# Attention scores as 64-row matmuls of split q and k, two heads in turns on the two row halves, in a hybrid decoder trunk

## The chip, the cores and the metric

One Trainium2 chip, one core of it. The metric is device time of one execution in microseconds (us); the time before is the median of three runs. A profile is one more execution, with the hardware profiler on.

## What is computed

Two decoder layers over 512 tokens of width 1024, float32 in and out. In each layer: half a SwiGLU FFN, a token mixing, another half FFN, and a gated per-layer embedding. The change lies in the token mixing, whose three head groups read one projection of the normed input:

```python
def stick_breaking_attention(q, k, v):          # 4 heads x 64
    z = einsum('bqhd,bkhd->bhqk', qb, k) * scale
    log_beta = log_sigmoid(z)
    log_keep = where(mask, log_sigmoid(-z), 0.0)
    log_between = cumsum(log_keep, axis=3, reverse=True) - log_keep
    a = where(mask, exp(log_beta + log_between), 0.0)
    return einsum('bhqk,bkhd->bqhd', a, v)

def differential_attention(q, k, v, lam):       # 4 heads x 2 components x 64, v 128
    s = einsum('bqhcd,bkhcd->bchqk', qb, k) * scale
    pr = softmax(where(mask, s, -inf), axis=-1)
    attn = pr[:, 0] - lam * pr[:, 1]
    return einsum('bhqk,bkhe->bqhe', attn, v)

def causal_softmax_attention(q, k, v): ...      # 4 latent heads, 96 = 64 + 32 rotary

h = h + 0.5 * swiglu(rms_norm(h), ...)
h = h + concat(stick, diff, latent) @ w_out
h = h + 0.5 * swiglu(rms_norm(h), ...)
h = h + (p[i] @ w_ple_proj) * sigmoid(rms_norm(h) @ w_ple_gate)
```

## The kernel before

Activations stay transposed in SBUF, 128 channels by 512 tokens a tile, with the tokens in reverse order. A product of full precision is made of three fast matmuls (fp32r, one pass): every operand is split into a high part, rounded to fp32r (`whi`, `xh`), and the rest (`wlo`, `xl`), and `mm3` adds high x high, high x low and low x high in one PSUM bank. ScalarE mostly makes the high part, VectorE the low one. Matmuls of plain float32 operands take four passes; the profile has two instructions for each. Weights come in chunks of up to 512 KB on the DMA queue of SyncE (`raw<-in_wts`), two chunks ahead of their use, in one fixed order.

The token mixing is woven from generators ("threads"): `fill` runs the projections in the order `sb, df, sv, lat, dv, heads, o0, o2, pp, o6`; `scores` starts score stages, `values` takes finished weights, transposes them (`tr`) and joins them with v (`av`, `dav`). `weave` lets the first thread go on that a planner's clock (a table of costs: engines, 0.65 us a DMA plus 2.0 us until it lands) says can go on. That order is then the program: each engine runs its instructions in it. At most `WINDOW = 4` stages are under way, and score banks come from a pool of four PSUM banks (`bank2`).

A stage is one head and one tile of 128 queries `qt` (3, 2, 1, 0), which in the reversed order meets 128, 256, 384 or 512 keys. Stick-breaking heads (`sb_stage`): a mask on VectorE, two sigmoids on ScalarE (`run`, `beta`), a scan over `run`, and a product. Differential heads (`diff_stage`): two components, each masked (`e<-sc`), exponentiated, and combined.

Scores contract over only 64 channels. Before, the array's 128 rows hold the high part of q on 64 rows and the low part on the other 64; k's high part stands on both halves (`khh`) and so does its low part (`kll`). Two matmuls of 128 rows then give (qh+ql)(kh+kl):

```python
self.nc.tensor.matmul(o, qs[:, q0:q0 + P], khh[:, q0:], start=True, stop=False)
self.nc.tensor.matmul(o, qs[:, q0:q0 + P], kll[:, q0:], start=False, stop=True)
```

For that layout the stick-breaking heads are moved inside SBUF by DMA (`qs<-qh`, `kdup<-kh` and so on: 24 moves of 64 rows a layer, issued by SyncE). The differential heads go through DRAM: the projections' output columns are sorted so that a tile of 128 rows has 16 channels of all 8 components; the tiles are stored (`scratch<-dh`, `scratch<-dl`), and five loads a head (`dops<-scratch`, into three of five buffers of the pool `pairs`) bring q stacked and k twice. In `scores()`, loads of a head are issued one head before its first stage.

SyncE issues every one of these transfers in program order, and waits in it: a load whose buffer is still in use holds up the weight chunks behind it.

Of the kernel before, what the change touches and what calls it, by code (L numbers as in the profile page):

```python
# [87 lines left out]
def _layer_weights(z, l):  # L88

    def kt(w):  # L90
        return w.reshape(-1, P, w.shape[1]).transpose(1, 0, 2)

    gu = {1: kt(z['w_ffn1_gu'][l]), 2: kt(z['w_ffn2_gu'][l])}
    dn = {1: kt(z['w_ffn1_down'][l]), 2: kt(z['w_ffn2_down'][l])}


    order = (64 * np.arange(8)[None, :] + np.arange(64)[:, None]).reshape(-1)
    cols = np.arange(z['w_in'].shape[2])
    cols[768:1792] = 768 + np.concatenate([order, 512 + order])
    win, wout = kt(z['w_in'][l][:, cols]), kt(z['w_out'][l])  # L100
    pp, pg = kt(z['w_ple_proj'][l]), kt(z['w_ple_gate'][l])
    uq = z['mla_w_uq'][l].reshape(256, 4, 96)
    rot = uq[:, :, 64:].reshape(256, 2, 2, 2, 16).transpose(0, 1, 3, 2, 4)
    uq = kt(np.concatenate([uq[:, :, :64].reshape(256, 256), rot.reshape(256, 128)], axis=1))
    ukv = z['mla_w_ukv'][l].reshape(P, 4, 128)
    ukv = np.concatenate([ukv[:, :, :64].reshape(P, 256), ukv[:, :, 64:].reshape(P, 256)], axis=1)
    sv = np.concatenate([win[:, :, 512:768], win[:, :, 2688:2720]], axis=2)
    parts = []
    for key, cols in PLAN:
        t = key[0]  # L110
        if t in 'gv':
            c = key[2] * P + (FF if t == 'v' else 0)
            w = gu[key[1]][:, :, c:c + P]
        elif t == 'dn':
            _, n, lo, m, half = key
            k0, k1 = (lo, lo + 6) if half == 0 else (lo + 6, lo + 11)
            w = dn[n][:, k0:k1, m * P:(m + 1) * P]
        elif t == 'in':
            w = win[:, :, key[1]:key[1] + P]
        elif t == 'sv':  # L120
            w = sv[:, key[1]:key[2]]
        elif t == 'dv':
            w = win[:, key[1]:key[2], 1792:2304]
        elif t == 'uq':
            w = uq
        elif t == 'ukv':
            w = ukv
        elif t == 'out':
            _, k0, k1, m0, m1 = key
            w = wout[:, k0:k1, m0 * P:m1 * P]  # L130
        elif t == 'pp':
            w = pp[:, :, key[1] * P:key[2] * P]
        else:
# [18 lines left out]
def _constants():  # L152
    c = np.zeros((P, 8), np.float32)
    for r in range(P):
        c[r, 0] = INV_D[r % 64 // 8]
# [161 lines left out]
class Body:  # L317
# [371 lines left out]
                        yield 'go'  # L689
        return banks  # L690

    def stack_q(self, st, kind, q, h0):

        qh, ql = self.t2(dt=F32R, name='qh'), self.t2(dt=F32R, name='ql')
        self.split(qh, ql, q)

        def move():
            yield from self.when(qh, ql)
            for h in range(2):
                rows = slice(64 * h, 64 * h + 64)  # L700
                t = self.t2(dt=F32R, name='qs')
                self.move(t[0:64], qh[rows])
                self.move(t[64:128], ql[rows])
                st['q', kind, h0 + h] = t
        self.spawn(move())

    def stack_k(self, st, kind, k, h0):

        parts = self.t2(dt=F32R, name='kh'), self.t2(dt=F32R, name='kl')
        self.split(parts[0], parts[1], k)  # L710

        def move():
            yield from self.when(*parts)
            for h in range(2):
                rows = slice(64 * h, 64 * h + 64)
                dup = []
                for p in parts:
                    t = self.t2(dt=F32R, name='kdup')
                    self.move(t[0:64], p[rows])
                    self.move(t[64:128], p[rows])  # L720
                    dup.append(t)
                st['k', kind, h0 + h] = dup
        self.spawn(move())

    def scores(self, st, kind, h, qt):
        while ('q', kind, h) not in st or ('k', kind, h) not in st:
            yield 'blocked'
        qs, (khh, kll) = st['q', kind, h], st['k', kind, h]
        yield from self.when(qs, khh, kll)
        yield from self.room('bank2')  # L730
        ps = self.bank2('sc', hold=True)
        q0 = qt * P
        o = ps[:, 0:S - q0]
        self.nc.tensor.matmul(o, qs[:, q0:q0 + P], khh[:, q0:], start=True, stop=False)
        self.nc.tensor.matmul(o, qs[:, q0:q0 + P], kll[:, q0:], start=False, stop=True)
        return o

    def transposed(self, at, qt, a):

# [129 lines left out]

    def diff_qk(self, l, x, st):  # L870

        st['scratch'] = s = self.dram.tile([2, 2, 64, 8, S], F32, name='scratch', tag='scratch')
        for m in range(4):
            for i, c in enumerate((768, 1280)):
                box = []
# [10 lines left out]
    def store(self, s, m, i, parts, st):  # L886
        yield from self.when(*parts)
        for p, t in enumerate(parts):
            self.move(s[i, p, 16 * m:16 * m + 16].rearrange('d c t -> (d c) t'), t)
        st['stored'] = st.get('stored', 0) + 1  # L890

    def diff_ops(self, st, h):


        s, hc = st['scratch'], slice(2 * h, 2 * h + 2)
        a, b = slice(0, 64), slice(64, P)
# [4 lines left out]
        for c in range(2):  # L901
            st['q', 'df', 2 * h + c], st['k', 'df', 2 * h + c] = q[:, c], (kh[:, c], kl[:, c])

    def out_proj(self, l, k0, k1, mixed, nxt=None):
        step = 8 // (k1 - k0)
# [36 lines left out]
                yield 'go'  # L942


    def sb_stage(self, st, h, qt):
        nc = self.nc
        n = S - qt * P
        z = yield from self.scores(st, 'sb', h, qt)
        nc.vector.tensor_tensor(out=z[:, 0:P], in0=z[:, 0:P], in1=self.m_strict, op=ALU.add)
        run, beta = self.st2(name='run')[:, 0:n], self.st2(name='beta')[:, 0:n]  # L950
        self.act(run, z, AF.Sigmoid, scale=-0.125)
        self.act(beta, z, AF.Sigmoid, scale=0.125)
        self.done(z)

        yield from self.when(run)
        nc.vector.tensor_tensor_scan(run, run, run, 1.0, ALU.mult, ALU.min)
        yield from self.when(beta)
        nc.vector.tensor_tensor(out=beta[:, 1:n], in0=beta[:, 1:n], in1=run[:, 0:n - 1], op=ALU.mult)
        st['weights', 'sb', h, qt] = beta

    def diff_stage(self, st, l, h, qt):
        nc = self.nc
        n = S - qt * P
        z = []
        for c in range(2):
            ps = yield from self.scores(st, 'df', 2 * h + c, qt)
            z.append(self.masked(ps, n, 0.125))
# [128 lines left out]
    def mixing(self, l, norm, nxt):  # L1096
# [4 lines left out]
        def start():  # L1101
            r = None
            for c in range(4):
# [6 lines left out]
                (self.stack_q, self.stack_k)[c // 2](st, 'sb', t, 2 * (c % 2))  # L1110

            st['rope'] = []
            for tab in self.rope_d:
# [30 lines left out]
                self.done(banks[t])  # L1144
            st['dv'] = dv

        stages = [(kind, h, qt) for kind in KINDS for h in range(4) for qt in (3, 2, 1, 0)]
        under_way = []

        def scores():  # L1150

            for kind, h, qt in stages:
                while len(under_way) >= WINDOW:
                    yield 'blocked'
                if kind == 'sb':
                    stage = self.sb_stage(st, h, qt)
                elif kind == 'df':
                    while st.get('stored') != 8:
                        yield 'blocked'
                    for i in range(min(h + 2, 4) if qt == 3 else 0):  # L1160
                        if ('q', 'df', 2 * i) not in st:
# [12 lines left out]

        def values():

            for kind, h, qt in stages:
                while ('weights', kind, h, qt) not in st:
                    yield 'blocked'
                if qt == 3:  # L1180
                    at = self.quad(dt=F32, name='at')
                yield from self.transposed(at, qt, st.pop(('weights', kind, h, qt)))
                under_way.pop(0)
                yield 'go'
                if qt == 0:
                    if kind == 'df':
                        finish = self.diff_finish(st, h, at)
                    elif h % 2 == 0:
                        even = at
                        continue  # L1190
                    else:
                        finish = self.join_heads(st, h - 1, (even, at), 'vs' if kind == 'sb' else 'vm',
                                                 0 if kind == 'sb' else 6)
                    self.spawn(finish, values)
                    yield 'go'

# [98 lines left out]
```

## Time and profile before

| what | value |
|---|---|
| median of 3 runs | 2057.83 us (2054.44 to 2058.54) |
| profiled execution | 2062.05 us |
| span of that profile | 2060.2 us |
| TensorE matmuls busy | 2029.0 us, 98% |
| VectorE busy | 1112.5 us, 54% |
| ScalarE busy | 793.1 us, 38% |
| mean DMA rate | 107 GB/s |
| mixing, layer 0 | about 369 to 613 us of the span |
| mixing, layer 1 | about 1385 to 1629 us of the span |

The profiled execution's own time has 1.85 us around the span. Names in the rows are tiles: `sc` a score bank, `pt` a projection into transposed layout, `pn` one into natural layout (values), `tr` a transpose of weights, `wo` the output projection, `msc` a latent head's score. All instructions go through one recording helper, so all have its line (L238), and DMA issues have L447 or L455. The start of a matmul is recorded, and its end is modelled with the array's latency in it, so that the time a matmul takes is read as the distance from its start to the start of the next one. fp32r shows as f32 in the matmuls' rows.

### The profile page before, as it was taken

The numbers are of one execution on the slowest core, as the hardware profiler recorded it, in microseconds if no ns is written. First come the engines' busy times: TensorE is split into PE (matmuls) and PEld (weight loads), VectorE is DVE, ScalarE is ACT, GpSimd is POOL, SyncE is SP. The second block draws the span as 40 slices with busy tenths as digits, with TensorE's granted clock in tenths as the row PEclk, the third lists the DMA queues.
The fourth block names the chain that finished last, engine by engine and source line by source line (L and its number), as shares of the span: only waits on it lengthen the run. The fifth ranks groups of instructions, "written<-read, shape, count | busy, mean of one in ns | idle before, by whom it ended". The sixth has DMA issues, their size and how long they took to land.

```text
span 2060.2 us, 23527 instructions
## 1 busy us (share of the span) xinstructions
PE 2029.0 (98%) x9148; PEld 1656.6 (80%) x9148; DVE 1112.5 (54%) x1762; ACT 793.1 (38%) x1275; POOL 5.1 (0%) x13
## 2 busy tenths in 40 slices
PE   8999999999999999999999999999999999999997
PEld 6888888887778888888888888888776788888885
DVE  6743444677756443444754334457686654344446
ACT  5422333445654222333543223335466433222343
POOL 0000000000000000000000000000000000000000
PEclk9999999999999999999999999999999999999998
DMA  4323233565323323333333233336633232333232
GB/s 167 101 86 108 94 94 91 156 193 142 92 87 92 98 85 107 99 90 97 101 95 100 85 110 92 93 102 175 191 110 104 81 103 90 91 106 103 85 107 75
DMA packets 73663, 220.34 MB, mean 107 GB/s; under 512 B 9024, under 2 KB 9024, under 8 KB 73552
## 3 DMA queue, kind: packets, MB, share of 16 engines
q1 hardware_dynamic: 73040, 217.23, 35.2%
q0 software_dynamic: 512, 1.61, 0.3%
q8 instruction: 72, 1.18, 0.2%
q14 instruction: 39, 0.32, 0.1%
HBM read 197.83 MB, written 10.49 MB: 101 GB/s over the span
## 4 chain that ended last, share of the span: by engine, by line
PE 93%; DMA 3%; DVE 2%; ACT 1%; issue 0%; SPq 0%; DVEq 0%
PE g L238 23%; PE v L238 23%; PE dn L238 23%; PE pt L238 6%; PE pg L238 4%; PE wo L238 3%; PE pn L238 2%; PE sc L238 1%; PE tr L238 1%; DMA dops<-scratch 1%; PE pp L238 1%; PE av L238 1%; DMA raw<-in_wts 1%; PE msc L238 1%; PE dav L238 1%; PE sum L238 1%
## 5 line engine op out<-in xcount | busy, mean ns | idle before, releaser
L238 ACT CAST whi<-raw 128x1024 fp32r<-128x1024 f32 (+3 forms) x363 | 346.1, 954 | 950.6 <-PE dn L238 295.2
L238 DVE TENSOR_TENSOR wlo<-raw,whi 128x1024 fp32r<-128x1024 f32 (+2 forms) x388 | 427.9, 1103 | 223.3 <-ACT whi L238 222.6
L238 PE MATMUL g<-xh,whi 128*128 128x512 f32 x704 | 276.8, 393 | 6.5 <-ACT xh L238 6.5
L238 PE MATMUL g<-xl,whi 128*128 128x512 f32 x704 | 274.9, 390 | 0.5 <-DVE xl L238 0.5
L238 PE MATMUL g<-xh,wlo 128*128 128x512 f32 x704 | 274.7, 390 | 0.0
L238 PE MATMUL v<-xh,whi 128*128 128x512 f32 x704 | 273.9, 389 | 0.0
L238 PE MATMUL v<-xh,wlo 128*128 128x512 f32 x704 | 273.9, 389 | 0.0
L238 PE MATMUL v<-xl,whi 128*128 128x512 f32 x704 | 273.9, 389 | 0.0
L238 PE MATMUL dn<-hh,whi 128*128 128x512 f32 x704 | 273.9, 389 | 0.0
L238 PE MATMUL dn<-hl,whi 128*128 128x512 f32 x704 | 273.9, 389 | 0.0
L238 PE MATMUL dn<-hh,wlo 128*128 128x512 f32 x704 | 273.9, 389 | 0.0
L238 DVE TENSOR_TENSOR v<-v,rt 128x512 f32<-128x512 f32 x88 | 60.8, 690 | 260.8 <-PE v L238 260.8
L238 PEld LDWEIGHTS g<-xh,whi 128*128 128x128 f32 x704 | 132.7, 188 | 35.0 <-ACT xh L238 6.8
L238 PEld LDWEIGHTS g<-xl,whi 128*128 128x128 f32 x704 | 132.7, 189 | 29.9 <-DVE xl L238 1.3
L238 PEld LDWEIGHTS g<-xh,wlo 128*128 128x128 f32 x704 | 132.6, 188 | 27.5
L238 PEld LDWEIGHTS dn<-hl,whi 128*128 128x128 f32 x704 | 132.2, 188 | 27.5
L238 PEld LDWEIGHTS v<-xh,wlo 128*128 128x128 f32 x704 | 132.2, 188 | 27.6 <-DVE wlo L238 0.2
L238 PEld LDWEIGHTS v<-xl,whi 128*128 128x128 f32 x704 | 132.2, 188 | 27.5
L238 PEld LDWEIGHTS dn<-hh,whi 128*128 128x128 f32 x704 | 132.2, 188 | 27.4
L238 PEld LDWEIGHTS v<-xh,whi 128*128 128x128 f32 x704 | 132.2, 188 | 27.3
L238 PEld LDWEIGHTS dn<-hh,wlo 128*128 128x128 f32 x704 | 132.2, 188 | 27.3
L238 DVE TENSOR_TENSOR g<-g,rt 128x512 f32<-128x512 f32 x88 | 60.8, 690 | 172.1 <-PE g L238 172.0
(196 smaller groups left out, 2581.7 us busy)
## 6 DMA issues: line engine op xcount, KB each, us to landing
raw<-in_wts SPq DMA_DIRECT2D x250, 512.0 KB, 3.5
raw<-in_wts SPq DMA_DIRECT2D x66, 384.0 KB, 3.0
raw<-in_wts SPq DMA_DIRECT2D x64, 320.0 KB, 2.9
dops<-scratch SPq DMA_DIRECT2D x32, 256.0 KB, 4.9
scratch<-dh SPq DMA_DIRECT2D x16, 256.0 KB, 2.9
scratch<-dl SPq DMA_DIRECT2D x16, 256.0 KB, 3.8
dops<-scratch SPq DMA_DIRECT2D x8, 512.0 KB, 7.6
res<-in_xT SPq DMA_DIRECT2D x8, 256.0 KB, 5.3
```

Source lines behind the costliest of these rows:

```text
L238: r = f(*args, **kw)
```

## The change

The scores of two stick-breaking heads (a pair), or of the two components of a differential head, are made together. q and k are split as before, but nothing is stacked: the two heads stand on rows 0 to 63 and 64 to 127 of the same four tiles `qh, ql, kh, kl`. Each score is three matmuls of 64 rows, qh kh, qh kl and ql kh, and the two heads take turns, each on its own half of the rows and into its own bank. The term ql kl is no longer made.

```diff
-    def stack_q(self, st, kind, q, h0):
...
-    def stack_k(self, st, kind, k, h0):
...
+    def split_pair(self, st, which, kind, pair, t):
+        parts = self.t2(dt=F32R, name=which + 'h'), self.t2(dt=F32R, name=which + 'l')
+        self.split(*parts, t)
+        st[which, kind, pair] = parts
+
+    def scores(self, st, kind, pair, qt):
...
+        (qh, ql), (kh, kl) = st['q', kind, pair], st['k', kind, pair]
+        yield from self.when(qh, ql, kh, kl)
+        while len(self.held['bank2']) > BANKS['bank2'] - 2:
+            yield 'blocked'
         q0 = qt * P
-        o = ps[:, 0:S - q0]
-        self.nc.tensor.matmul(o, qs[:, q0:q0 + P], khh[:, q0:], start=True, stop=False)
-        self.nc.tensor.matmul(o, qs[:, q0:q0 + P], kll[:, q0:], start=False, stop=True)
-        return o
+        out = []
+        for i in range(2):
+            yield from self.room('bank2')
+            out.append(self.bank2('sc', hold=True)[:, 0:S - q0])
+        for p, (q, k) in enumerate(((qh, kh), (qh, kl), (ql, kh))):
+            for i, o in enumerate(out):
+                rows = slice(64 * i, 64 * i + 64)
+                self.nc.tensor.matmul(o, q[rows, q0:q0 + P], k[rows, q0:], start=p == 0, stop=p == 2)
+        return out
```

The 24 moves a layer are gone. The scratch tensor is now ordered by component first, the columns of `w_in` are sorted to fit, and a differential head has two tiles (q, k) with the high part in one half of the columns and the low part in the other, filled by four loads of 256 KB:

```diff
-        st['scratch'] = s = self.dram.tile([2, 2, 64, 8, S], F32, name='scratch', tag='scratch')
+        st['scratch'] = s = self.dram.tile([2, 2, 8, 64, S], F32, name='scratch', tag='scratch')
...
-        q, kh, kl = (self.pairs.tile([P, 2, S], F32R, name='dops', tag='pr') for _ in range(3))
-        self.move(q, s[0, :, :, hc].rearrange('p d c t -> (p d) c t'))
-        for t, half, p in ((kh, a, 0), (kh, b, 0), (kl, a, 1), (kl, b, 1)):
-            self.move(t[half], s[1, p, :, hc])
+        for i, which in enumerate('qk'):
+            t = self.pairs.tile([P, 2, S], F32R, name='dops', tag='pr')
+            for p in range(2):
+                self.move(t[:, p], s[i, p, 2 * h:2 * h + 2].rearrange('c d t -> (c d) t'))
+            st[which, 'df', h] = t[:, 0], t[:, 1]
```

A stick-breaking stage now does a pair (mask and sigmoids of both, then scan and product of both), counts as two in the window of four, and `values` transposes both heads of it before it frees its place.

On TensorE, the first scores of layer 0 (`pt` is the projection of the stick-breaking k and of the first differential tile). Before, the high halves of one head's four stages, and a few matmuls later the low halves:

```order
L238 MATMUL pt<-xh,wlo 128x512
L238 MATMUL sc<-kdup,qs 128x128
L238 MATMUL sc<-kdup,qs 128x256
L238 MATMUL sc<-kdup,qs 128x384
L238 MATMUL sc<-kdup,qs 128x512
L238 MATMUL pt<-xh,whi 128x512
```

and in the changed kernel two pair stages, one directly behind the other (x2 is one matmul of each head):

```order
L240 MATMUL pt<-xh,wlo 128x512
L240 MATMUL sc<-kh,qh 128x128 x2
L240 MATMUL sc<-kl,qh 128x128 x2
L240 MATMUL sc<-kh,ql 128x128 x2
L240 MATMUL sc<-kh,qh 128x256 x2
L240 MATMUL sc<-kl,qh 128x256 x2
L240 MATMUL sc<-kh,ql 128x256 x2
L240 MATMUL pt<-xh,whi 128x512
```

The pair's scores stand some 30 `pt` matmuls earlier than the first scores did. In the whole program the 48 pair stages stand in 36 unbroken blocks: 12 of them are directly behind another.

On VectorE, behind the second block of that first pair (384 and 512 keys), in the changed kernel: the split of the last stick-breaking k, a weight chunk and the two rotary tables (`rot`) come first, then masks (`sc<-sc`), scans (`run<-run`) and products (`beta`) of both heads:

```order
L240 TENSOR_TENSOR sbqk<-pt,rt 128x512
L240 TENSOR_TENSOR wlo<-raw,whi 128x1024
L240 TENSOR_TENSOR kl<-sbqk,kh 128x512
L240 TENSOR_TENSOR rot<-cos_427,rt 128x512
L240 TENSOR_TENSOR rot<-sin_425,rt 128x512
L240 COPY rt<-rt 128x4
L240 TENSOR_TENSOR sc<-sc,cst 128x128 x2
L240 SCALAR_TENSOR_TENSOR run<-run 128x384
```

Before, one head's scans of 128, 256 and 384 keys follow each other in this place, with the `rot` rows ahead of the first of them.

On SyncE's queue, from the last store of the differential q and k on. Before (64x1024 is half a tile of k):

```order
L447 DMA dops<-scratch 128x1024
L447 DMA scratch<-dh 128x512
L455 DMA raw<-in_wts 128x1024
L447 DMA scratch<-dl 128x512
L447 DMA dops<-scratch 64x1024 x4
L447 DMA dops<-scratch 128x1024
L447 DMA dops<-scratch 64x1024 x4
L455 DMA raw<-in_wts 128x1024 x2
```

and now:

```order
L449 DMA dops<-scratch 128x512 x2
L449 DMA scratch<-dh 8x16x512
L457 DMA raw<-in_wts 128x1024
L449 DMA scratch<-dl 8x16x512
L449 DMA dops<-scratch 128x512 x6
L457 DMA raw<-in_wts 128x1024
L449 DMA dops<-scratch 128x512 x2
L457 DMA raw<-in_wts 128x1024
L449 DMA dops<-scratch 128x512 x4
```

Behind the last store, nine loads stood ahead of the next weight chunk, the last two of them into a buffer that the first head still read; now six stand there, all into free buffers, and the four of the last row (k of the third head, q of the fourth) wait for the first head's.

## Rows read from the trace of the kernel before

**Rows 1.** The page: busy time by engine, and the chain that ended last by engine.

```profile
PE 2029.0 (98%) x9148; PEld 1656.6 (80%) x9148; DVE 1112.5 (54%) x1762; ACT 793.1 (38%) x1275; POOL 5.1 (0%) x13
...
PE 93%; DMA 3%; DVE 2%; ACT 1%; issue 0%; SPq 0%; DVEq 0%
```

**Rows 2.** Groups by line and shape, TensorE: stick-breaking score matmuls of one width.

```profile
L238 PE MATMUL sc<-kdup,qs 128*128 128x512 f32 x16 | 5.9, 428 | 0.0
```

**Rows 3.** Timeline of TensorE around the first scores: start us, us, instruction.

```profile
396.72 0.80 PE L238 MATMUL sc<-kdup,qs 128*128 128x128 f32 x4
397.36 0.39 PE L238 MATMUL pt<-xh,whi 128*128 128x512 f32 x1
```

**Rows 4.** Timeline of TensorE: differential heads' values, four heads of 128 output columns.

```profile
530.06 8.80 PE L238 MATMUL dav<-at,dv 128*128 128x512 f32 x32
538.61 0.48 PE L238 MATMUL uq<-ch,whi 128*128 128x512 f32 x1
```

**Rows 5.** Timeline of TensorE: latent values, two heads of 64 output columns in turns.

```profile
573.15 0.40 PE L238 MATMUL wo<-mh,wlo 128*128 128x512 f32 x1
573.47 2.38 PE L238 MATMUL av<-at,vm 128*64 128x512 f32 x16
575.78 0.50 PE L238 MATMUL wo<-mh,whi 128*128 128x512 f32 x1
576.12 0.39 PE L238 MATMUL wo<-ml,whi 128*128 128x512 f32 x1
```

**Rows 6.** Timelines of TensorE, 10 ns and then 3 us: four matmuls of 32 rows.

```profile
556.31 0.70 PE L238 MATMUL drr<-rt,cst 32*128 32x512 f32 x2
...
556.31 1.98 PE L238 MATMUL drr<-rt,cst 32*128 32x512 f32 x8
```

**Rows 7.** Timelines of TensorE and its weight loads, inside a full-array stretch.

```profile
542.56 0.39 PE L238 MATMUL uk<-ch,wlo 128*128 128x512 f32 x1
542.78 0.28 PE L238 MATMUL uv<-whi,ch 128*128 128x256 f32 x1
...
542.56 0.19 PEld L238 LDWEIGHTS uv<-whi,ch 128*128 128x128 f32 x1
```

**Rows 8.** Timelines of TensorE: waits for differential loads, layer 0, then layer 1.

```profile
460.35 3.08 PE L238 MATMUL sc<-dops 128*128 128x128 f32 x12 [1.77 <-DMA dops<-scratch]
...
488.00 0.41 PE L238 MATMUL sc<-dops 128*128 128x128 f32 x2 [1.86 <-DMA dops<-scratch]
...
1476.68 0.70 PE L238 MATMUL sc<-dops 128*128 128x128 f32 x4 [0.43 <-DMA dops<-scratch]
1479.51 3.86 PE L238 MATMUL sc<-dops 128*128 128x128 f32 x12 [2.13 <-DMA dops<-scratch]
...
1505.63 0.41 PE L238 MATMUL sc<-dops 128*128 128x128 f32 x2 [0.56 <-DMA dops<-scratch]
```

**Rows 9.** Busy time by stretch: PE, PEld, DVE, ACT, POOL; granted clock; DMA share; GB/s.

```profile
460.00:466.00 6.00, 5.65 (x25) 5.14 (x26) 3.46 (x16) 1.81 (x8) 0.00 (x0) 0.72 0.78 201
488.00:494.00 6.00, 6.00 (x25) 5.37 (x26) 3.40 (x16) 4.18 (x14) 0.00 (x0) 0.72 0.64 141
1479.00:1484.00 5.00, 4.49 (x18) 4.24 (x19) 3.54 (x15) 0.20 (x1) 0.00 (x0) 0.66 0.48 103
```

**Rows 10.** The chain that ended last, 440 to 500 us: start us, us, what.

```profile
445.00 1.28 ACT L360
...
448.22 0.69 DVE dl L238
...
448.93 5.96 DMA scratch<-dl
...
455.45 4.77 DMA dops<-scratch
```

**Rows 11.** Timelines: TensorE's wait for a stick-breaking product, and VectorE's scans.

```profile
405.47 0.52 PE L238 MATMUL tr<-cst,beta 128*128 128x128 f32 x3 [0.38 <-DVE beta L238]
...
403.71 0.95 DVE L238 TENSOR_TENSOR_SCAN run<-run 128x384 f32<-128x384 f32 x1
```

More of the change, by code (lines that the diff above doesn't have):

```diff
@@ L94, in _layer_weights @@
     dn = {1: kt(z['w_ffn1_down'][l]), 2: kt(z['w_ffn2_down'][l])}
-    order = (64 * np.arange(8)[None, :] + np.arange(64)[:, None]).reshape(-1)
+    order = [64 * np.arange(8)[:, None] + d + np.arange(n)[None, :] for d, n in
+             ((0, 8), (8, 8), (16, 16), (32, 16), (48, 16))]
+    order = np.concatenate([o.reshape(-1) for o in order])
     cols = np.arange(z['w_in'].shape[2])
@@ L154, in _constants @@
     for r in range(P):
-        c[r, 0] = INV_D[r % 64 // 8]
+        c[r, 0] = INV_D[r % 8]
         c[r, 1] = -1.0 if r < 64 else 1.0
@@ L690, in proj_n @@
         return banks
-    def stack_q(self, st, kind, q, h0):
[L694 to L705, printed above, removed]
@@ L707, in stack_k @@
-    def stack_k(self, st, kind, k, h0):
[L709 to L723, printed above, removed]
@@ L725, in scores @@
-    def scores(self, st, kind, h, qt):
-        while ('q', kind, h) not in st or ('k', kind, h) not in st:
+    def split_pair(self, st, which, kind, pair, t):
[3 more added lines that the diff above has]
+    def scores(self, st, kind, pair, qt):
+        while ('q', kind, pair) not in st or ('k', kind, pair) not in st:
             yield 'blocked'
[L728 to L731, printed above, removed]
+        (qh, ql), (kh, kl) = st['q', kind, pair], st['k', kind, pair]
+        yield from self.when(qh, ql, kh, kl)
+        while len(self.held['bank2']) > BANKS['bank2'] - 2:
+            yield 'blocked'
@@ L888, in store @@
         for p, t in enumerate(parts):
-            self.move(s[i, p, 16 * m:16 * m + 16].rearrange('d c t -> (d c) t'), t)
+            if m == 0:
+                self.move(s[i, p, :, 0:8], t[0:64])
+                self.move(s[i, p, :, 8:16], t[64:128])
+            else:
+                self.move(s[i, p, :, 16 * m:16 * m + 16], t)
         st['stored'] = st.get('stored', 0) + 1
     def diff_ops(self, st, h):
-        s, hc = st['scratch'], slice(2 * h, 2 * h + 2)
-        a, b = slice(0, 64), slice(64, P)
-        q, kh, kl = (self.pairs.tile([P, 2, S], F32R, name='dops', tag='pr') for _ in range(3))
-        self.move(q, s[0, :, :, hc].rearrange('p d c t -> (p d) c t'))
-        for t, half, p in ((kh, a, 0), (kh, b, 0), (kl, a, 1), (kl, b, 1)):
-            self.move(t[half], s[1, p, :, hc])
-        for c in range(2):
-            st['q', 'df', 2 * h + c], st['k', 'df', 2 * h + c] = q[:, c], (kh[:, c], kl[:, c])
+        s = st['scratch']
+        for i, which in enumerate('qk'):
[3 more added lines that the diff above has]
+            st[which, 'df', h] = t[:, 0], t[:, 1]
     def out_proj(self, l, k0, k1, mixed, nxt=None):
@@ L942, in ple_proj, with sb_stage @@
                 yield 'go'
-    def sb_stage(self, st, h, qt):
+    def sb_stage(self, st, pair, qt):
         nc = self.nc
         n = S - qt * P
[L948 to L959, printed above, removed]
+        banks = yield from self.scores(st, 'sb', pair, qt)
+        sticks = []
+        for z in banks:
+            nc.vector.tensor_tensor(out=z[:, 0:P], in0=z[:, 0:P], in1=self.m_strict, op=ALU.add)
+            run, beta = self.st2(name='run')[:, 0:n], self.st2(name='beta')[:, 0:n]
+            self.act(run, z, AF.Sigmoid, scale=-0.125)
+            self.act(beta, z, AF.Sigmoid, scale=0.125)
+            self.done(z)
+            sticks.append((run, beta))
+        for i, (run, beta) in enumerate(sticks):
+            yield from self.when(run)
+            nc.vector.tensor_tensor_scan(run, run, run, 1.0, ALU.mult, ALU.min)
+            yield from self.when(beta)
+            nc.vector.tensor_tensor(out=beta[:, 1:n], in0=beta[:, 1:n], in1=run[:, 0:n - 1], op=ALU.mult)
+            st['weights', 'sb', 2 * pair + i, qt] = beta
     def diff_stage(self, st, l, h, qt):
@@ L963, in diff_stage @@
         n = S - qt * P
[L964 to L967, printed above, removed]
+        banks = yield from self.scores(st, 'df', h, qt)
+        z = [self.masked(ps, n, 0.125) for ps in banks]
         sm, r = self.sm(2, name='sum'), self.sm(2, name='rec')
@@ L1109, in start @@
                 nc.vector.tensor_tensor(out=t, in0=box[0], in1=r, op=ALU.mult)
-                (self.stack_q, self.stack_k)[c // 2](st, 'sb', t, 2 * (c % 2))
+                self.split_pair(st, 'qk'[c // 2], 'sb', c % 2, t)
             st['rope'] = []
@@ L1145, in diff_v @@
             st['dv'] = dv
-        stages = [(kind, h, qt) for kind in KINDS for h in range(4) for qt in (3, 2, 1, 0)]
+        stages = [(kind, h, qt) for kind in KINDS for h in range(2 if kind == 'sb' else 4) for qt in (3, 2, 1, 0)]
         under_way = []
@@ L1152, in scores @@
             for kind, h, qt in stages:
-                while len(under_way) >= WINDOW:
+                while sum(1 + (k == 'sb') for k, _, _ in under_way) >= WINDOW:
                     yield 'blocked'
@@ L1160, in scores @@
                     for i in range(min(h + 2, 4) if qt == 3 else 0):
-                        if ('q', 'df', 2 * i) not in st:
+                        if ('q', 'df', i) not in st:
                             self.diff_ops(st, i)
@@ L1175, in values @@
         def values():
[L1177 to L1182, printed above, removed]
+            ats = {}
+            for kind, i, qt in stages:
+                for h in ((2 * i, 2 * i + 1) if kind == 'sb' else (i,)):
+                    while ('weights', kind, h, qt) not in st:
+                        yield 'blocked'
+                    if qt == 3:
+                        ats[h] = self.quad(dt=F32, name='at')
+                    yield from self.transposed(ats[h], qt, st.pop(('weights', kind, h, qt)))
                 under_way.pop(0)
                 yield 'go'
-                if qt == 0:
+                if qt == 0 and (kind == 'df' or h % 2 == 1):
                     if kind == 'df':
[L1187 to L1190, printed above, removed]
-                    else:
-                        finish = self.join_heads(st, h - 1, (even, at), 'vs' if kind == 'sb' else 'vm',
-                                                 0 if kind == 'sb' else 6)
+                        finish = self.diff_finish(st, h, ats.pop(h))
+                    else:
+                        finish = self.join_heads(st, h - 1, (ats.pop(h - 1), ats.pop(h)),
+                                                 'vs' if kind == 'sb' else 'vm', 0 if kind == 'sb' else 6)
                     self.spawn(finish, values)
```

## The prediction

> **What bounds the kernel now.** I read the page first. TensorE's matmuls are busy for 98% of the span, and the chain that ended last lies on TensorE for 93% of it [rows 1]. So a change pays only what it takes from TensorE's own stream of matmuls, or from the places where that stream waits. I therefore looked for the price of the score matmuls (the groups by shape and the timeline around them), for what a change of tile shape costs in this trace (the stretches where other matmuls already use part of the array), and for TensorE's waits in the two mixing stages with their granted clock. What the other engines do is read only where TensorE waits for them.
>
> **1. The score matmuls.** The stick-breaking heads have 16 of each width [rows 2], the differential ones with eight components instead of four heads twice as many, so there are 48 sets of the four widths (a set: the high or the low half of one head's four stages). One set took 397.36 - 396.72 = 0.64 us on TensorE, with plain matmuls right ahead and behind [rows 3]. Before, that is 48 x 0.64 = 30.7 us. Afterwards each of the 24 pairs of heads or components (2 stick-breaking and 4 differential a layer, so 12 over both layers) needs three sets for each of its two heads, 72 sets in all. If the two row halves run side by side, they take the time of 36: 23.0 us, **7.7 us less**. If they do not, 72 x 0.64 = 46.1 us, 15.4 us more.
>
> Do they run side by side? The trace has no 64-row matmul, but two near ones. In the latent values two heads use 64 columns each in turns: 16 instructions in 575.78 - 573.47 = 2.31 us [rows 5]; one differential head of the same lengths at full width took (538.61 - 530.06)/4 = 2.14 us [rows 4]. Two heads cost about as much as one. And the four 32-row matmuls of the sub-norm, nearest in kind, started two within 10 ns and ended after 1.98 us [rows 6]; one 512-wide plain matmul is 2.14 x 512/1280 = 0.86 us, so four in sequence would be 3.4 us. I take full overlap.
>
> **2. Going into and out of the split array.** This has a price in the same rows. The matmul ahead of the `av` block takes 573.47 - 573.15 = 0.32 us and the one behind it 0.34 us [rows 5], where a matmul in a plain stretch takes 542.78 - 542.56 = 0.22 us [rows 7]; the block itself is 2.31 - 2.14 = 0.17 us too long. Together 0.10 + 0.12 + 0.17 = 0.39 us for each visit. The `drr` block gives 1.98 - 2 x 0.86 = 0.26 us inside alone. The 48 pair stages stand in 36 unbroken blocks, so I add 36 x 0.39 = **14.0 us**. Bounds: 0.17 us a visit if only the inner part is paid (6.1 us), 0.50 us if the wider weights of 128 columns show twice (18 us). That this is more than the matmuls save is the main point against the change.
>
> Does a weight load still hide inside a block, where each half gets new weights for every pass? In a plain stretch the next weights start loading at 542.56 while a matmul over the same 128 rows starts in that very instant, and the next matmul follows 0.22 us later [rows 7]: hidden. The Trainium skill says otherwise (TensorE: Matmul & The Clock Gate, Part 3, "The mechanism"): a weight load overlaps a matmul in flight only where their row groups differ. By that, the second and third pass of each half would wait for their own load; the price of it is worked out as a rival. The sum goes by the row.
>
> **3. Waits for the differential loads.** TensorE stood 1.77 + 1.86 + 0.43 + 2.13 + 0.56 = 6.75 us for `dops<-scratch` [rows 8]. After three of these waits its granted clock fell from 2.4 to 1.2 GHz for a while: the mean was 0.72 over 6 us twice and 0.66 over 5 us once [rows 9], which cost 1.7 us each time, 5.1 us in all. So late loads cost 11.8 us.
>
> The waits are of two kinds. The 1.86 and the 0.56 are the third head's: with three of five buffers to a head, its last tile could only be loaded when the second head was done. With two tiles a head its q finds a free buffer and its k needs only the first head's, one head of work earlier. These 2.4 us, and one fall of the clock, go. The others are the first head's. The chain to them ran through a table load on ScalarE (1.28), the low half of the last projection, its store (5.96 from issue to landing) and the load of k's low part (4.77) [rows 10]. Now the stick-breaking stages are over sooner and the table load stands ahead of the last projections; k's low part is one transfer of 256 KB instead of two, and 256 KB less is in flight beside the store (an estimate from the 5.96: 1 us off). That is 1.3 + 0.5 + 1 = 2.8 us off a chain that was 1.8 us late. But about nine transposes that stood between the last projection and these scores are gone too, so TensorE arrives about 1 us sooner. Balance: just in time. I leave 0.5 us a layer and no fall of the clock: **10.8 us less**. Bounds: 11.8 (no wait), 4.1 (the first head as late as before: 2.4 + 1.7).
>
> The 24 moves a layer that go were not waited for by TensorE (other matmuls filled the time, [rows 3] shows scores right behind projections); I give them nothing. Fewer matmuls' operands, the extra halves of two stores a layer and the finer planner window cost nothing that a row shows: TensorE has projections in front of every one of those.
>
> **4. The stick-breaking chain.** Before, TensorE waited 0.38 us for a product (`beta`) once a layer; VectorE's scan of 384 keys alone takes 0.95 us [rows 11]. Now both heads' scans and products follow each other, twice the work between a pair's scores and its last transpose, and for the second block of the first pair VectorE first does five full-width instructions (`dl` of that width takes 0.69 us [rows 10]; a weight chunk is twice as wide), some 4 us. TensorE has 12 projections, 12 x 0.22 = 2.7 us, before it wants the first of these products. In the second pair many more projections stand between. I expect two waits of under 1 us in each layer, **2.4 us more** in all than now. Bounds: 0 (VectorE catches up) and 6.
>
> **Sum:** -7.7 + 14.0 - 10.8 + 2.4 = -2.1 us. The profiled execution's own time is 2062.05 us (its span 2060.2 and 1.85 around it), so 2060.0; it was 4.2 us slower than the median of the runs, 2057.83, which gives 2055.7 us. About 0.2% (4.1 us) is what a measurement of this kernel can tell from no change.
>
> **Rivals.**
> *The switches cost less.* If only the inner 0.17 us is paid where weights for the other half are loaded ahead, the second term is 6.1: -10.0 us, 2047.8. For it: the 0.10 and 0.12 in [rows 5] may belong to the change from fast to plain matmuls, which scores don't make. Against: `drr` with plain matmuls on its outer side still shows 0.26 inside.
> *The first head's loads stay late.* Place: the first `dops` scores of each layer. They keep 1.77 + 0.43 + 2.13 us and two falls of the clock, 7.7 instead of 1.0: +4.6 us, 2062.4, slower. It decides once k's low part lands some 2 us after TensorE comes.
> *The pair's scans hold up TensorE.* 3 us of waits a layer and a fall of the clock each (1.7): 9.4 instead of 2.4, +4.9 us, 2062.7.
> *The halves do not overlap.* +15.4 instead of -7.7: +21 us, 2078.8. [rows 6] speak against it.
> *Weights wait for their own half.* Two of three loads in 48 stages and two heads side by side, each at most the 0.19 us of a load in [rows 7]: up to 96 x 0.19 = 18 us more, 2074. This is what the Trainium skill's rule above would do; [rows 7] contradict it.
>
> **How the numbers follow.** Chances: the sum as forecast 0.52, with a range of its own of 2051 to 2061 from the bounds of the terms 3 and 4 (0.18 of it faster, 0.34 within 0.2%); cheaper switches 0.20 (faster); late loads 0.12 (0.05 the same, 0.07 slower); scans 0.08 (0.02 and 0.06); no overlap 0.05; weights 0.03. Faster 0.38, same 0.41, slower 0.21. The range from 2046 to 2065 takes in the first four cases and leaves the last two and the tails, under 2 in 10.
>
> **What the profile of the changed kernel would show.** Term 1: the two heads' score matmuls start within some 10 ns, and the six of 512 keys take about 0.7 us. Term 2: the matmul ahead of a block and the first behind it take about 0.3 instead of 0.22 us. Term 3: no wait for `dops` over 1 us, none at all at the third head, and no stretch at the lower clock in the mixing. Term 4: short waits of transposes for `beta` behind the first pair's second block. I am wrong if blocks cost clearly other than 0.4 us, if scores run one half after the other, or if new waits bring the clock down.

## The result, and the profile after

The changed kernel took 2070.24 us (median of 4 runs, 2068.86 to 2070.45) where the one before took 2058.07 in the same comparison: ratio 1.0067, 95% interval 1.0055 to 1.0080. It is 12 us slower by these medians, 14 by the ratio, which is not the quotient of the two medians; the prediction said 2055.7 and its range ended at 2065. The profiled execution of the changed kernel took 2070.45 us, 8.4 more than that of the kernel before.

The page after, busy time of TensorE and the chain that ended last, as in [rows 1]:

```profile
PE 2033.9 (98%) x9244; PEld 1648.6 (80%) x9244; DVE 1112.1 (54%) x1752; ACT 799.5 (39%) x1285; POOL 5.1 (0%) x13
...
PE 93%; DVE 3%; DMA 2%; ACT 1%; issue 0%; SPq 0%; DVEq 0%
```

TensorE still sets the time, so again only its stream and its waits count. A block of stick-breaking scores of 512 keys between projections, timeline of TensorE (start us, us, instruction), answers to [rows 3, 5]:

```profile
424.37 0.40 PE L240 MATMUL pt<-xh,wlo 128*128 128x512 f32 x1
424.70 0.51 PE L240 MATMUL sc<-kh,qh 64*128 64x512 f32 x2
425.04 0.40 PE L240 MATMUL sc<-kl,qh 64*128 64x512 f32 x2
425.28 0.40 PE L240 MATMUL sc<-kh,ql 64*128 64x512 f32 x2
425.61 0.50 PE L240 MATMUL pt<-xh,whi 128*128 128x512 f32 x1
425.94 0.39 PE L240 MATMUL pt<-xl,whi 128*128 128x512 f32 x1
```

Read the starts. Each line of scores is both heads' matmul of one pass, and the middle pass takes 425.28 - 425.04 = 0.24 us, the time of one full-width matmul: the halves run side by side. The matmul ahead takes 0.33, the block 425.61 - 424.70 = 0.91, the matmul behind 0.33; three passes and two matmuls of 0.23 would be 1.15, so the visit costs 0.42 us.

The waits of TensorE in the whole run (us in total, times, longest), which answer to [rows 8, 11]:

```profile
PE sc L240 <- DMA dops<-scratch: 4.7, 2, 2.4
PE sc L240 <- issue: 3.5, 2, 2.1
PE tr L240 <- DVE beta L240: 1.6, 4, 0.6
PE av L240 <- DVE vs L240: 0.8, 2, 0.4
...
PE sc L240 <- DVE nm L240: 0.5, 2, 0.2
```

The third head no longer waits for a load (only 0.5 us for `nm`). But the first head does, for 4.7 + 3.5 = 8.2 us over both layers, where all heads together stood 6.75 us before. The "issue" in the second line I count with them: it is the pause just before the same first scores, for which the profile names no releaser. The timelines of TensorE in layer 0 and layer 1:

```profile
461.81 0.33 PE L240 MATMUL sc<-dops 64*128 64x128 f32 x2 [1.38 <-issue]
464.44 1.01 PE L240 MATMUL sc<-dops 64*128 64x128 f32 x6 [2.30 <-DMA dops<-scratch]
...
1483.73 0.39 PE L240 MATMUL sc<-dops 64*128 64x128 f32 x2 [2.14 <-issue]
```

And the stretches behind these waits by busy time, columns as in [rows 9]:

```profile
464.44:470.10 5.66, 5.66 (x29) 4.41 (x29) 2.72 (x15) 3.34 (x13) 0.00 (x0) 0.50 0.78 294
1486.40:1490.68 4.28, 4.15 (x22) 3.65 (x24) 1.52 (x10) 2.54 (x11) 0.00 (x0) 0.50 0.90 335
```

The granted clock was 0.50 in both, 1.2 GHz, while TensorE was busy for 5.66 and 4.15 us: half of that, 2.8 + 2.1 = 4.9 us, was lost, about the 5.1 of the profile before. (The clock fell before the waits ended, but what TensorE waits out costs nothing more at the lower clock.) The chain that ended last shows why the loads were late; it answers to [rows 10]:

```profile
446.48 6.06 DMA scratch<-dl
...
454.16 6.89 DMA scratch<-dl
...
461.07 3.33 DMA dops<-scratch
...
464.44 1.44 PE sc L240 x7
```

Two stores stand in it now. The first (q's low half) took 6.06 us to land. SyncE's next instruction but one, the load of that data, waited for it, and behind that load stood the last two stores of k. So the last store was issued at 454.16, only 6.3 us before TensorE came (460.43, which is 461.81 less the wait of 1.38); before it had been 9.6 us (448.93 and 458.58, which is 460.35 less the wait of 1.77, [rows 8, 10]). And then it took 6.89 us itself. The data of that store was ready sooner than it was issued; VectorE's timeline:

```profile
451.12 0.68 DVE L240 TENSOR_TENSOR dl<-dp,dh 128x512 fp32r<-128x512 f32 x1
```

From its end at 451.80 the store waited 2.4 us in SyncE's queue, where before it set off at once (448.22 + 0.69 and 448.93). So of the 3.4 us of head start that the store lost, 2.4 are the queue's, and 1.0 is that TensorE came that much sooner after the data.

### The profile page after: what moved, and what is told of

Its sections match the earlier page's. It is cut to its first block, busy times and chain, and to the rows that moved or that the text cites. A ratio compares the mean times of both kernels' runs of the same rounds, so it can differ in the third digit from the quotient of the medians.

```text
span 2068.4 us, 23602 instructions
## 1 busy us (share of the span) xinstructions
PE 2033.9 (98%) x9244; PEld 1648.6 (80%) x9244; DVE 1112.1 (54%) x1752; ACT 799.5 (39%) x1285; POOL 5.1 (0%) x13
## 2 busy tenths in 40 slices
DMA packets 70526, 209.84 MB, mean 101 GB/s; under 512 B 7936, under 2 KB 7936, under 8 KB 70416
## 4 chain that ended last, share of the span: by engine, by line
PE 93%; DVE 3%; DMA 2%; ACT 1%; issue 0%; SPq 0%; DVEq 0%
PE g L240 23%; PE v L240 23%; PE dn L240 23%; PE pt L240 6%; PE pg L240 4%; PE wo L240 3%; PE pn L240 2%; PE sc L240 1%; DMA scratch<-dl 1%; PE tr L240 1%; PE pp L240 1%; PE av L240 1%; PE msc L240 1%; PE dav L240 1%; PE sum L240 1%; DVE wlo L240 1%
## 5 line engine op out<-in xcount | busy, mean ns | idle before, releaser
L240 ACT CAST whi<-raw 128x1024 fp32r<-128x1024 f32 (+2 forms) x369 | 351.5, 952 | 978.2 <-PE dn L240 291.3
```

The lines of the kernel that those rows point to most:

```text
L240: r = f(*args, **kw)
```

## The experiments

**The theory (A)**: a store whose access pattern has 8 as its outer count (8x16x512: component, dimension, token) is spread over 8 of the 16 DMA engines, lands late, and drags the first differential head's loads, TensorE and its clock with it. **The rival (B)**: the loss is the price of the split array and the scans, and the late loads only stand where another limit would be. All times are medians, beside runs of the kernel before on the same chip (2054.7 to 2055.7 us).

**1. The change with stores of 16 rows** (`e1_16rows`). The projection's columns go back to the old order, and the store's loops are turned:

```diff
-            if m == 0:
-                self.move(s[i, p, :, 0:8], t[0:64])
-                self.move(s[i, p, :, 8:16], t[64:128])
-            else:
-                self.move(s[i, p, :, 16 * m:16 * m + 16], t)
+            self.move(s[i, p, :, 16 * m:16 * m + 16].rearrange('c d t -> d c t'), t)
```

> The changed kernel with the projection's rows in the old order (dimension ahead of component), so that each store to scratch has an outer count of 16 (16x8x512) instead of 8 (8x16x512); layout, loads and scores as in the change. Theory A (the stores with an outer count of 8 use 8 of the 16 DMA engines, land late, and with them the first differential head's loads): a lone store lands in about 3 us instead of 6, up to 16 packets in flight instead of 8, TensorE's waits ahead of the first differential scores fall from 9.1 us over both layers to 2 to 4, and the time is 2060 to 2065. Theory B (the loss is the switching of the array and the scans, and the loads' lateness only moves about): stores faster, time within 2 us of the change's 2070.2.

Measured: 2060.55 us, ratio 1.0022 (1.0013 to 1.0032), so by the ratios about 9 us of the change's loss are gone; by the distances from the medians of before beside each, 12.2 and 5.7 us, it is 6.5 (the two comparisons ran on different chips). The busy time by microsecond, with the busy share of the 16 DMA engines in the last column but one, first of the change:

```profile
443.00:444.00 1.00, 1.00 (x6) 0.81 (x6) 0.06 (x1) 0.29 (x1) 0.00 (x0) 1.00 0.57 201
444.00:445.00 1.00, 1.00 (x6) 0.84 (x5) 0.97 (x2) 0.97 (x2) 0.00 (x0) 1.00 0.51 157
445.00:446.00 1.00, 1.00 (x6) 0.82 (x5) 1.00 (x2) 0.29 (x1) 0.00 (x0) 1.00 0.49 167
```

And of this kernel, at the same store:

```profile
442.00:443.00 1.00, 1.00 (x6) 0.81 (x5) 0.00 (x0) 0.00 (x0) 0.00 (x0) 1.00 1.00 367
443.00:444.00 1.00, 1.00 (x6) 0.84 (x5) 0.18 (x1) 0.41 (x1) 0.00 (x0) 1.00 0.95 352
444.00:445.00 1.00, 1.00 (x7) 0.81 (x6) 0.97 (x2) 0.97 (x2) 0.00 (x0) 1.00 0.06 21
```

The change's stores keep half of the engines busy without a pause; those of 16 rows use all of them and are done. The chain that ended last here:

```profile
451.89 5.64 DMA scratch<-dl
...
457.59 4.01 DMA dops<-scratch
```

And the wait at its end, on TensorE's timeline:

```profile
461.64 0.85 PE L238 MATMUL sc<-dops 64*128 64x128 f32 x10 [1.07 <-DMA dops<-scratch]
```

The last store is issued 2.3 us sooner and lands 1.2 us faster; the waits for `dops` are 1.7 us over both layers and the clock stays at 2.4 GHz in the mixing (1.00 over 380 to 620 and 1380 to 1640 us). Theory A, with the size it gave; this last store still took 5.6 us, among loads and a weight chunk. Scattered rows in DRAM are not the cause: these stores scatter them more finely (single rows of 2 KB) than the change's did (16 rows in one piece).

**2. The kernel before with such stores** (`e3_before_8rows`): the scores and loads of before, with the change's order of columns and `rearrange('d c t -> c d t')` in the store.

> The kernel before, scores and loads untouched, with the rows of the differential projection component-major as in the change, so that each store to scratch has an outer count of 8. Theory A (stores with an outer count of 8 use 8 DMA engines and land late): stores land in 5 to 7 us instead of 2.5 to 3, the first differential scores of both layers wait 3 us longer each and the clock falls behind them, time 2061 to 2068 against 2055 of before in the last comparison. Theory B (a late store costs only together with the change's two loads for q): 2054 to 2058.

Measured: 2068.51 us, ratio 1.0066 (1.0051 to 1.0081): 13.8 us from the stores alone, Theory A, just above its range. Its waits for `dops` are 11.4 us, and its chain:

```profile
443.64 5.59 DMA scratch<-dl
...
450.85 7.60 DMA scratch<-dl
...
458.96 4.42 DMA dops<-scratch
```

The pages also count the DMA packets under 512 B: 9024 in the kernel before and 8832 here, 8128 in experiment 1 and 7936 in the change, each time 192 fewer with the stores of 8. If every DMA engine ends its part of a store with one such packet (an assumption here), 32 stores on 16 engines make 512 of them, and 40 on 8 engines (the first tile of a projection is stored in two halves) make 320: 192 fewer.

**3. The two parts apart** (`e4_sb_only`, `e5_df_only`): in each, the functions of the other kind are those of the kernel before.

> The kernel before with the stick-breaking part of the change alone; differential part as before. By the terms measured in the change's trace: a third of the gain on the scores (-2.6 us), 12 to 16 visits of 0.41 us to the split array (+5 to +6.5), waits for the scan of both heads (+2 to +3): 2062 to 2066. If the whole loss lay in the differential loads: 2056 to 2059.

> The kernel before with the differential part of the change alone; stick-breaking part as before, with its moves. By the terms: scores -5.1 us, 20 to 24 visits of 0.41 us (+8 to +10), third head's wait gone (-4), first head's waits and clock +7 to +8: 2064 to 2068. If the loads' lateness came from the stick-breaking part's earlier arrival of TensorE, the first head waits less than 5 us over both layers here: 2058 to 2061.

Measured: 2059.48 us, ratio 1.0021 (1.0012 to 1.0031), and 2065.81, ratio 1.0050 (1.0033 to 1.0066): +4.6 and +11.0 us. Both parts lose; the differential one is inside its range, the stick-breaking one falls between its two and is met by neither. The stick-breaking one has 12 visits, 12 x 0.42 = 5.0 us for 2.6 saved, and waits for `beta` of 1.7 us against 0.8. The differential one waits 3.8 + 2.4 us at its first head, so the late loads don't come from the other part.

**4. Later scores by the planner** (`e2_land8`): the change with one number altered, so that the planner thinks the differential loads land at 8 us and puts other work ahead of the first scores.

```diff
-                self.move(t[:, p], s[i, p, 2 * h:2 * h + 2].rearrange('c d t -> (c d) t'))
+                self.move(t[:, p], s[i, p, 2 * h:2 * h + 2].rearrange('c d t -> (c d) t'), 8.0)
```

> The changed kernel with one number of the planner altered: it takes the differential loads to land 8 us after their issue slot instead of 2, so it puts the first differential scores behind more projection work; stores stay slow. Theory A (TensorE waits for the first differential head, and its clock falls for it): the waits of 9.1 us and the fall of the clock of 6.8 us there are mostly gone, time 2056 to 2062. Theory B (the waiting only stands in for another limit): the waits reappear at the transposes or at the weights behind, time 2067 to 2071.

Measured: 2079.58 us, ratio 1.0113 (1.0098 to 1.0128), worse than either theory said. The waits for `dops` are gone, but TensorE stands 10.9 us for `vs`. The chain that ended last, in layer 0:

```profile
446.51 5.89 DMA scratch<-dl
...
453.52 6.04 DMA raw<-in_wts
...
459.66 1.06 ACT whi L240
...
461.89 0.34 DVE pe L240 x2
462.23 5.97 DMA raw<-in_wts
...
468.30 1.04 ACT whi L240
```

And TensorE's timeline at its end:

```profile
469.95 1.12 PE L240 MATMUL av<-at,vs 128*64 128x512 f32 x2 [5.65 <-ACT vs L240]
```

A weight chunk (453.52) stands in SyncE's queue behind the load that waits for q's slow store, and takes 6.04 us to land, where the page of the kernel before has a median of 3.5 for 512 KB. The next one (462.23) sets off when VectorE has read an earlier chunk out of its buffer and six more loads in the queue (from 458.31, 3.82 us) are through, and takes 5.97. ScalarE waits for its data with the copies to `vs` behind it, and TensorE for those. The delay moved from the scores to the weights. How much of it is the order of the queue and how much the slow landing of the chunks, this run doesn't take apart.

**5. The loads by another queue** (`e8_pool_loads`): the change, slow stores included, with `dops` loaded by `gpsimd.dma_start`.

> The change as it is, slow stores and all, with the differential loads issued by GpSimd's queue instead of SyncE's; the order on TensorE is the same. Theory A1 (part of the lateness is SyncE's order: the loads for q, waiting for a slow store, hold back the last two stores for k): those stores issue about 2 us sooner, the first differential scores wait 9.1 us less 4 over both layers, time 2062 to 2067. Theory A2 (the landing of the stores alone decides): waits as in the change within 1 us, time 2068 to 2072.

Measured: 2071.37 us, ratio 1.0074 (1.0061 to 1.0088), waits 8.6 us. Its chain:

```profile
452.34 6.75 DMA scratch<-dl
459.09 1.69 issue
460.78 3.38 DMA dops<-scratch
```

The last store is issued 1.8 us sooner and lands 2.0 us sooner than in the change (459.09 against 461.05), as A1 said; but GpSimd issues the load only 1.69 us after that, a pause for which the profile shows no cause. So SyncE's order did cost 2 us of the chain, and the pause lost them again. The time and the waits are those of A2; whether A1's time would have come without the pause is open.

**6. One half after the other** (`e6_serial`): experiment 1 with the loops over heads and passes exchanged. The order of the instructions on TensorE, a block of 128 keys:

```
1671 L238 MATMUL sc_2767<-kh_2744,qh_2670 128x128
1672 L238 MATMUL sc_2767<-kl_2745,qh_2670 128x128
1673 L238 MATMUL sc_2767<-kh_2744,ql_2671 128x128
1674 L238 MATMUL sc_2768<-kh_2744,qh_2670 128x128
```

> The change with 16-row stores (2060.5), but the six score matmuls of a block in the order A A A B B B instead of A B A B A B, A and B the row halves. The planner makes fewer visits of it in its order: 26 instead of 36 (-4.1 us at 0.41). Theory A (the halves overlap only for neighbours in different halves): a block of 512 columns takes 0.65 us more, 384 0.5, 256 0.33, 128 about 0: +18 us, time 2073 to 2077. Theory B (matmuls of one half overlap with the other's wherever they stand in the block): 2055 to 2059.

Measured: 2062.61 us, ratio 1.0035 (1.0022 to 1.0048). The block of 512 keys, timeline of TensorE:

```profile
424.77 0.51 PE L238 MATMUL sc<-kh,qh 64*128 64x512 f32 x2
425.11 0.41 PE L238 MATMUL sc<-kl,qh 64*128 64x512 f32 x2
425.35 0.40 PE L238 MATMUL sc<-kh,ql 64*128 64x512 f32 x2
425.68 0.50 PE L238 MATMUL pt<-xh,whi 128*128 128x512 f32 x1
```

It is the block of the change to the hundredth: the second head's first matmul, fourth in order, starts with the first head's first. This run's Theory A is refuted, and so is the prediction's rival that the halves don't overlap. Its Theory B has the mechanism, but the time is 4 to 8 us over what it gave; waits for `dops` (2.8), `nm` (1.0) and `pe` (1.5) are longer here than in experiment 1 (1.7, 0.5 and none), and the clock fell twice where there it didn't (a mean of 0.66 over 463 to 468 us and of 0.57 over 559 to 563, 1.7 us each).

**7. More visits** (`e7_visits`): experiment 1 with a pause of the thread between the three passes, so that projections come between them.

```diff
+            if p < 2:
+                yield self.nc.clock.now['PE'] + 0.01
```

> The change with 16-row stores (2060.5), with the three steps of a score block emitted apart, so that full-array work of the projections comes in between: 114 visits to the split array instead of 36 by the order of the instructions. Theory A (each visit costs 0.41 us, as read off the matmuls' distances in the change's trace): +32 us, 2088 to 2096. Theory B (the distances are read wrong, and a visit is cheap): below 2070. In between, the difference over 78 is the price of a visit.

Measured: 2099.96 us, ratio 1.0218 (1.0203 to 1.0233): +39.4 over experiment 1, so Theory A, though 4 us above its range. One pass on its own, on TensorE's timeline:

```profile
406.40 0.40 PE L238 MATMUL pt<-xh,wlo 128*128 128x512 f32 x1
406.73 0.50 PE L238 MATMUL sc<-kh,qh 64*128 64x512 f32 x2
407.16 0.50 PE L238 MATMUL pt<-xh,whi 128*128 128x512 f32 x1
407.50 0.40 PE L238 MATMUL pt<-xl,whi 128*128 128x512 f32 x1
```

And a stretch at a lower clock that is new here, by busy time (1614:1628 of layer 1 has the same 0.63):

```profile
576.00:590.00 14.00, 11.34 (x37) 6.82 (x37) 9.27 (x24) 8.39 (x21) 0.54 (x1) 0.63 0.17 56
```

Here 0.33 + 0.43 + 0.34 = 1.10 us stand for three times 0.23: 0.41 a visit. The clock takes up to 2 x 14 x 0.37 = 10.4 us of the 39.4, and TensorE's listed waits add up to 21.7 us instead of 16.7; the other 24 over 78 visits are 0.31 each, 29 with the waits left in are 0.37. So the total shows that visits cost, and roughly how much; the 0.41 is read off the starts.

**8. A faster version** (`b_df16m`, its twin `b_df16`, and both in five rounds): the stick-breaking part as before, the differential part of the change with 16-row stores; merged, the tiles of 128 and 256 keys share a bank and a visit.

```diff
+GROUPS = ((3, 2), (1,), (0,))
+        for qt in qts:
+            out.append([b[:, at:at + S - qt * P] for b in banks])
+            at += S - qt * P
```

> A try at a faster version: stick-breaking part as before with its moves; differential part of the change with 16-row stores, and the scores of the last two query tiles (128 and 256 columns) in one bank, so that 16 visits are left of 24. Terms against before: scores -5.1, visits +6.6, third head's wait gone and first head's shorter (-2 to -5): 2050 to 2056. If the loads' lateness is not cured by the stores, 2060 and above.

> Stick-breaking part as before, differential part of the change with 16-row stores: 20 visits, no merging of query tiles. Against the merged version beside it: 4 visits of 0.42 us more, +1.7 us: 2053 to 2056. Against the differential part alone with the change's stores (2065.8 where before took 2054.9): -9 to -12 us, which is what the stores cost.

> The merged version again, in more rounds, beside its unmerged twin: 2051 to 2054 where before takes 2054 to 2055; a lone gain under 0.1% would leave it open whether it beats before.

Measured: merged 2052.34 us, ratio 0.9990 (0.9980 to 1.0000), and again 2052.54, ratio 0.9984 (0.9975 to 0.9993); unmerged 2055.26, ratio 0.9999 (0.9990 to 1.0007). Four visits fewer gave 2.7 us, more than the 1.7 that they cost by themselves. Against the differential part with the change's stores the unmerged one is 10.5 us faster (on another chip). The merged one's differential scores have almost no wait left, as their group by line shows (idle time last):

```profile
L238 PE MATMUL sc<-dops 64*128 64x128 f32 (+3 forms) x192 | 20.1, 338 | 0.4 <-DMA dops<-scratch 0.3
```

And the clock stays up there, by busy time:

```profile
455.00:470.00 15.00, 14.33 (x98) 10.39 (x99) 12.38 (x41) 8.17 (x26) 0.00 (x0) 1.00 0.78 271
```

It beats the kernel before by 2.4 and 3.1 us in the two comparisons, and the change, which ran on another chip, by some 15 to 18.

## Why the prediction was wrong

**Term 1, the score matmuls (-7.7): right.** The halves overlap, in both orders that were tried (experiment 6). (The prediction says 24 pairs once; the sum goes by the right 12, with 24 heads or components.)

**Term 2, the visits (+14.0): right.** 36 x 0.42 = 15.1 us, read off the change's block and confirmed by experiment 7 and, roughly, by the merging. The rival of cheaper switches is out. So is that of weights that wait for their own half. The weight loads of the block of 512 keys shown above:

```profile
424.81 0.19 PEld L240 LDWEIGHTS sc<-kl,qh 64*128 64x128 f32 x2
425.05 0.19 PEld L240 LDWEIGHTS sc<-kh,ql 64*128 64x128 f32 x2
```

The second pass's weights are loaded from 424.81 to 425.00, while the first pass on the same rows (from 424.70, the next one from 425.04) is in flight, and the third's from 425.05 on, with the second pass; the passes still follow at 0.24 us. The Trainium skill's rule (TensorE: Matmul & The Clock Gate, Part 3, "The mechanism"), that a load overlaps only where row groups differ, does not hold here.

**Term 4, the scans (+2.4): right in kind.** Waits for `beta` went from 0.8 to 1.6 us, and `av` waits 0.8 for `vs`, which it did not: +1.6.

**Term 3, the loads (-10.8): the step that failed**, at "2.8 us off a chain that was 1.8 us late ... Balance: just in time. I leave 0.5 us a layer and no fall of the clock". The half on the third head came true. For the first head I took the store's landing from a row of a store with another access pattern, and let it get 1 us faster. It got slower: q's store 6.06 us and k's 6.89, and through SyncE's order, which the prediction's chain did not have, k's store also set off later. In layer 0, on the wait of 1.77 us before: 2.4 us in SyncE's queue, 1.0 because TensorE came sooner after the data, 0.9 for the slower store, less 1.4 for the load of k's low part (3.33 instead of 4.77) and 0.5 for the gap between store and load, make 4.2; from TensorE's arrival (460.43) to the scores that waited last (464.44) it was 4.0. The waits became 8.2 + 0.5 instead of 1.0 us, and the clock cost 4.9 us instead of none. This is the rival "the first head's loads stay late", to which I gave 0.12 and 2062.4: its place was right, its size not, since it had the loads stay as late as before. Experiments 1, 2 and 8 agree that the stores are the cause of it (6.5 to 9, 13.8 and 10.5 us). The change's diff showed it: the outer count of the store went from 128 rows in one piece to 8. And the Trainium skill says it (DMA: Bandwidth & Descriptors, "Why a DMA increments its semaphore by 16 and not by 1"): a copy issued by SyncE runs on the largest number of engines, up to 16, that divides the outermost dimension on both sides. The DMA shares of 0.49 to 0.57 against 0.95 to 1.00 in experiment 1 agree. The prediction did not apply it to the stores.

**A second error in the same term** is what the gain was measured against. The profile before held three falls of the clock, a granted mean of 0.994 and 2062.05 us; the 19 runs of before beside experiment 1 had granted means of 0.996 to 0.998 and a median of 2054.86. Experiment 1's profile has no fall in the mixing, and its mean is 0.997; 12 of the 19 runs have that or more. So most runs of before seem to lack those falls (only their means are known); the 5.1 us were then not there to be gained, and taking the difference of 4.2 us to the median off the sum did not repair this: it probably stands for the same falls.

**The sum after the fact**: -7.7 + 15.1 + (8.7 - 6.75) + (4.9 - 5.1) + 1.6 = +10.8 us between the two profiled executions, which differ by 8.4; for experiment 1 the same sum gives -0.6 (waits 2.2, no loss of clock, scans and `vs` 1.7) and -2.2 was measured (2059.81 against 2062.05). Between the median runs 5.1 us less of clock on the side of before make experiment 1's sum +4.5; measured +5.7. So the sums hold to some 2 us, and 2.4 us of the changed kernel's I could not place.

## What to carry to other kernels

When a layout in DRAM changes, look at the access pattern of every store and load that touches it, not at its bytes: in this case the outermost count of a store decided how many DMA engines carried it, and one that landed late also delayed what stood behind it in an in-order queue, weights included. A split of the array into row halves pays only in long blocks: at 0.42 us a visit, 36 visits ate twice the 7.7 us that the halves saved, and a block of 512 keys alone, four passes before and three now, saves one of 0.23. And before a gain is booked on a stall or a clock fall of one profile, check on the spread of the other runs that they have it too.

## What the runs showed of the hardware that was not expected

- Stores of 8x16x512 from SyncE kept the DMA share at 0.49 to 0.57 and took 5.6 to 7.6 us to land in the chains shown; as 16x8x512 of the same 256 KB they reached 0.95 to 1.00 and landed in a median of 3.0 (high halves) and 4.1 us (low ones), 5.6 in the chain.
- TensorE starts a matmul for one row half ahead of two earlier ones for the other half (experiment 6): the order A A A B B B ran like A B A B A B.
- A visit to the split array cost 0.41 us with one pass and 0.42 with three, in the two blocks shown: 0.10 at the matmul ahead, 0.2 inside and 0.1 at the one behind.
